# Fewer, longer vector operations and a new order for the opening of a Strassen-type matrix product on one core

## The chip, the core and the metric

The kernel runs on one core of one Trainium2 chip. The metric is the time of one execution on the device in microseconds. The engines of the core are named as the profile names them: PE (TensorE, the matmuls), DVE (VectorE), ACT (ScalarE), POOL (GpSimd) and SP (SyncE, which issues the DMAs here). They run side by side, each through its own list of instructions in order, and wait for each other by semaphores.

## The reference

```python
def reference(x, w):                       # x: 8 x 2048 x 2048, w: 2048 x 2048, float32
    cs = np.cumsum(x, axis=1)
    diff = cs - np.concatenate([zeros, cs[:, :-1, :]], axis=1)
    return np.matmul(diff, w).astype(np.float32)
```

The difference of the running sums is x itself up to rounding, so the kernel computes x times w: 16384 rows of 2048 by a 2048 x 2048 matrix.

## The kernel before

The rows of x are cut into 128 tiles of 128 rows. The depth of 2048 is cut into 16 pieces of 128 (`ko`), w into 32 pieces of 128 x 1024 floats, `w.h.ko` with h the half of the columns.

**The opening (period 0).** The first four row tiles (`PLAIN`) are multiplied plainly in bfloat16 while w arrives. Their x comes in 16 loads `first x.q.r` (depth quarter q, tile r, L249), is cast (`cast x.q.a`, a pair of tiles, L257), transposed on PE into a bank (`turn x.q.a`, L263) and copied out (`turned`, L275). Each weight piece is fetched (`w.h.ko`, L289), cast into a ring of seven buffers (`cast w.h.ko`, L310) and searched for its largest magnitude (`max w`, L297). `plain.h.r.ko` (L319) are the products; `part` takes a few of them early into a spare bank, and `left over` finishes those later. Ahead of the first products PE is given `WARM` matmuls on zeros (L358). The largest weight of all, `max`, `max of all` on POOL, `uw` and `uinv` (L447 to L454) gives one scale for the weights.

**The weights as sums.** With `uinv` the blocks B11, B21 and B22 of w (1024 x 1024 each) are stored as float16 over w's own place (`block`, L457), and the sums T1 = B12 - B11, T2 = B22 - T1, T3 = T2 - B11 and T4 = B21 - T2 are made on DVE, each in eight operations of 1024 elements (`difference` L538, `less` L581, called in `group_plain`). The place that a stored B12 would have serves as room for sums of quarters (`spare`). A second level cuts five of these blocks into quarters t11 to t22 and forms sums of quarters (`in1` to `in5`; `make_1` to `make_5`, L703 to L737), in four operations of 512 elements for each sum.

**The groups.** The other 124 tiles go in 31 groups of four. In a group the tiles g, g+1 and h = g+2, h+1 form two 2 x 2 block problems that are solved by seven products instead of eight (the names A11g, S1g, S2h and so on are blocks of x and their sums). The first group (`group_plain`, L817, period 0) uses the seven products directly. From the second on (`group`, L940, one period each), five of the products, P1 to P5, are themselves done by seven quarter products over the pair g, h (class `Quarters`, L743), with their own sums on DVE (`s1` to `s4`, `middle`, `last`) and copies on ACT (`first`, `out2`, `out4`). In the second group P1 is still done whole.

**In and out.** A row tile is loaded in two halves (`load`), its mean magnitude is found on ACT (`weigh`, `mean`) and inverted on DVE (`scale`), it is scaled to float16 on ACT (`narrow`) and transposed by a DMA (`turn`). Results are taken out of the PSUM banks by ACT (`keep`, with a scale, L617), added to by DVE (`add` and `add_one`, L629 and L633: one operation for each half of 512 columns) and stored by SP (`put`). PSUM is eight separate bank tiles, used in pairs.

**What sets the order.** `record` (L116) notes every operation under a label with its engine. At the end `emit` (L205) sorts all of them by a table `places`, written out in the file: the period times 1620 plus the label's number in the table of its period. The table has entries of its own for periods 0, 1, 2, 29, 30 and 31; all others use the entry `None`. The order on each engine, SP's queue of DMAs included, follows from that sort alone:

```python
def when(op):
    at, label = op[:2]
    own = places[at] if at in places else places[None]
    return at * PERIOD + own.get(label, 0)
```

## Time and profile before

| | us |
|---|---|
| runs | 1449.58, 1450.01, 1451.32 (median 1450.01) |
| span of the profiled execution, first to last instruction | 1449.2 |
| first product of the four plain tiles starts | 13.19 |
| DVE inverts the largest weight (`uinv`) | 60.77 |
| last matmul ends | 1444.13 |
| one group in the steady state | 44.03 |

The profiled execution gives its span alone; the runs were timed without the profiler. PE is busy for 99% of the span, DVE for 92%, ACT for 83%. A matmul row shows 0.38 us from its start to the end of its depth, but the next one starts 0.22 us after it; so a short hole between two matmuls does not show as idle time, and a longer one shows 0.16 us short. Likewise DVE and ACT operations that follow each other overlap by some 0.08 to 0.1 us. The lines of the profile stand in the prediction, where they are used.

### The profile page before, as it was taken

The page shows a single profiled execution, that of the slowest core. Times are in us where ns is not written, and L with a number is a line of the kernel's source. Part 1 is how long each engine was busy: PE and PEld are TensorE (multiplying, and loading weights), DVE is VectorE, ACT ScalarE, POOL GpSimd, SP SyncE. Part 2 cuts the span into 40 slices and gives each one's busy share as a digit, 9 for nine tenths or more (in the row PEclk, how much of TensorE's full clock was granted, in tenths as well). Part 3 has the DMA queues.
Part 4 walks back from the last instruction along what each step waited for, and adds up shares of the span by engine and source line. Part 5 has one row for each costly group of instructions (what it writes and reads, how often), then busy time and mean ns, then how long its engine had stood idle before and what let it go on. Part 6 is the DMA issues. An engine that isn't in the chain of part 4 may idle for free.

```text
span 1449.2 us, 20358 instructions
## 1 busy us (share of the span) xinstructions
PE 1438.6 (99%) x6692; PEld 652.2 (45%) x6698; DVE 1334.3 (92%) x2345; ACT 1204.5 (83%) x1994; POOL 0.5 (0%) x5
## 2 busy tenths in 40 slices
PE   8999999999999999999999999999999999999998
PEld 4444444444444444444444444444444444444443
DVE  6999999999999999999999999999999999999988
ACT  5997888898888888888988888988888888889783
POOL 0000000000000000000000000000000000000000
PEclk9999999999999999999999999999999999999999
DMA  9999979899888999989998888998989998989973
GB/s 360 369 252 272 252 212 228 240 247 262 226 234 226 243 262 231 244 222 228 247 265 233 228 229 237 252 257 226 222 239 244 260 248 225 218 236 248 264 200 116
DMA packets 343930, 351.59 MB, mean 243 GB/s; under 512 B 270992, under 2 KB 270992, under 8 KB 343824
## 3 DMA queue, kind: packets, MB, share of 16 engines
q1 hardware_dynamic: 343824, 350.29, 89.4%
q8 instruction: 52, 0.85, 0.2%
q14 instruction: 54, 0.44, 0.1%
HBM read 150.99 MB, written 134.22 MB: 197 GB/s over the span
## 4 chain that ended last, share of the span: by engine, by line
PE 91%; issue 4%; DMA 2%; ACT 2%; DVE 1%; DVEq 0%; POOLq 0%; ACTq 0%; SPq 0%
PE b L610 61%; PE b L588 30%; DMA x<-F 1%; DMA F<-in_x_dram 1%; DVE W L460 1%; ACT waste L140 0%; DMA out_dram<-arena 0%; ACT W L462 0%; DVE arena L635 0%; ACT arena L624 0%; ACT F L178 0%; ACT arena L342 0%; ACT arena L178 0%; DVE arena L576 0%; DVE W L576 0%
## 5 line engine op out<-in xcount | busy, mean ns | idle before, releaser
L588 PE MATMUL b<-W,x 128*128 128x512 f16 x2144 | 518.1, 379 | 0.1
L635 DVE SCALAR_TENSOR_TENSOR arena<-b,tiny,arena 128x512 f32<-128x512 f32 x612 | 446.9, 745 | 16.0 <-PE b L610 4.8
L610 PEld LDWEIGHTS <-arena 128*128 128x128 f16 x2744 | 268.2, 98 | 325.4 <-DVE arena L576 6.3
L610 PE MATMUL b<-W,arena 128*128 128x512 f16 x1672 | 413.7, 379 | 0.8 <-DVE arena L576 0.4
L624 ACT ACTIVATE arena<-b,tiny 128x512 f32<-128x512 f32 x496 | 317.0, 684 | 35.4 <-PE b L588 14.9
L588 PEld LDWEIGHTS <-x 128*128 128x128 f16 x2144 | 209.7, 98 | 253.3 <-issue 0.3
L140 ACT ACTIVATE waste<-F,tiny 128x1024 uint8<-128x1024 f32 x246 | 283.9, 1154 | 15.6 <-DMA F<-in_x_dram 14.1
L178 ACT ACTIVATE F<-F,tiny 128x1024 f16<-128x1024 f32 x246 | 282.1, 1147 | 10.9 <-DVE tiny L163 9.4
L610 PE MATMUL b<-W,x 128*128 128x512 f16 x1192 | 287.5, 379 | 0.0
L610 PE MATMUL b<-arena 128*128 128x512 f16 x1072 | 261.6, 379 | 0.0
L610 PEld LDWEIGHTS <-x 128*128 128x128 f16 x1428 | 139.7, 98 | 168.5
L576 DVE TENSOR_TENSOR b<-b,arena 128x512 f32<-128x512 f32 x298 | 205.9, 691 | 5.7 <-ACT arena L627 2.0
L627 ACT COPY b<-b 128x512 f32<-128x512 f32 x149 | 85.5, 574 | 134.4 <-PE b L610 112.4
L627 ACT COPY arena<-b 128x512 f32<-128x512 f32 x298 | 170.2, 580 | 19.9 <-PE b L610 13.0
L576 DVE TENSOR_TENSOR arena<-W 128x2048 f16<-128x2048 f16 (+1 forms) x158 | 185.6, 1176 | 0.4 <-PE b L610 0.4
L576 DVE TENSOR_TENSOR arena<-x,x 128x512 f16<-128x512 f16 (+1 forms) x181 | 91.5, 506 | 50.1 <-PE b L610 50.1
L576 DVE TENSOR_TENSOR x<-x,x 128x1024 f16<-128x1024 f16 x124 | 85.2, 687 | 2.0
L576 DVE TENSOR_TENSOR arena<-W,arena 128x512 f16<-128x512 f16 (+1 forms) x157 | 85.9, 563 | 0.6 <-PE b L610 0.5
L576 DVE TENSOR_TENSOR arena<-arena 128x512 f16<-128x512 f16 x120 | 50.8, 424 | 13.7 <-PE b L610 11.8
L610 PE MATMUL b<-arena,x 128*128 128x512 f16 x236 | 60.3, 379 | 0.0
L324 PE MATMUL b<-arena 128*128 128x512 bf16 x234 | 53.5, 379 | 1.5 <-DVE arena L279 0.8
L576 DVE TENSOR_TENSOR arena<-x,arena 128x512 f16<-128x512 f16 x119 | 49.6, 417 | 0.6 <-PE b L610 0.6
(49 smaller groups left out, 503.6 us busy)
## 6 DMA issues: line engine op xcount, KB each, us to landing
F<-in_x_dram SPq DMA_DIRECT2D x246, 512.0 KB, 5.4
out_dram<-arena SPq DMA_DIRECT2D x240, 512.0 KB, 4.8
W<-in_w_dram SPq DMA_DIRECT2D x31, 512.0 KB, 9.5
out_dram<-arena SPq DMA_DIRECT2D x31, 256.0 KB, 2.7
W<-in_x_dram SPq DMA_DIRECT2D x16, 256.0 KB, 6.6
x<-F SPq DMA_TRANSPOSE x246, 4.4
arena<-in_x_dram SPq DMA_DIRECT2D x2, 512.0 KB, 5.1
W<-in_w_dram SPq DMA_DIRECT2D x2, 256.0 KB, 9.0
```

The lines of the kernel that those rows point to most:

```text
L140: lambda: nc.scalar.activation(waste, data, ABS, bias=least, scale=1.0 / ROW, accum_out=m),
L178: lambda: nc.scalar.activation(to, data, COPY, scale=s),
L324: said = nc.tensor.matmul(to[n], xP[:, r, ko, :], b[:, ds(n * NB, NB)], start=(ko == 0), stop=(ko == KO - 1),)
L460: ask = lambda: nc.vector.tensor_scalar(to, src, uinv, None, MUL)
L576: record(label, "dve", lambda: nc.vector.tensor_tensor(dst, p, q, op))
L588: said = nc.tensor.matmul(to[n], a[k], b[k][:, n, :], start=(start and k == 0), stop=(k == KH - 1), skip_group_check=True,)
L610: said = nc.tensor.matmul(to, a[k], b[k], start=(start and k == 0), stop=(k == 3), skip_group_check=True)
L624: record(label, "act", lambda: nc.scalar.activation(c, p, COPY, scale=u))
L627: record(label, "act", lambda: nc.scalar.copy(to, p))
L635: label, "dve", lambda: nc.vector.scalar_tensor_tensor(c, p, u, c, MUL, ADD)
```

## The change

The diff has five parts.

1. The first-level sums T2, T3 and T4 take two depth pieces in one operation (four operations of 2048 elements in place of eight of 1024), and each sum of quarters takes the whole quarter (one operation of 2048 in place of four of 512). Additions to C take both halves in one operation of 1024 elements in periods 0 to 2, that is in the first three groups, and stay in halves from period 3 on. For this, PSUM becomes one tile of eight banks, and a pair of banks has a name for both.
2. Operations that copy or scale are recorded for either engine (`on_two`), and a list `moved` names those that change between ACT and DVE: 26 in period 0 (list below), and 3, 5 and 6 in periods 1, 2 and 3, all from ACT to DVE there.
3. Seven operations on the weights' quarters (in2, in3) stay in group 0 and nine (in1, in4, in5) in group 1, as before; the new functions `made` and `plainly` only restate when they are formed and which product is done whole (P1 of the second group, as before).
4. `WARM` is 24 in place of 30.
5. `places` has new tables for periods 0, 1 and 2 and one more for period 3, with the first loads in another order; 29, 30, 31 and `None` are as they were. The number of matmuls apart from the warm-ups is the same, and so is the number of DMAs.

```diff
-    WARM = 30
+    WARM = 24
...
-    banks = [psum.tile([P, NB], f32, name=f"b{i}") for i in range(8)]
-    pairs = [banks[2 * i : 2 * i + 2] for i in range(4)]
+    bank = psum.tile([P, 8, NB], f32, name="banks")
+    banks = [bank[:, i, :] for i in range(8)]
+
+    class Two(list):
+        def __init__(self, i):
+            super().__init__(banks[i : i + 2])
+            self.both = bank[:, ds(i, 2), :]
+
+    pairs = [Two(2 * i) for i in range(4)]
...
+    moved = {
+        0: (
+            "turned x.0.0", "cast w.0.0", "cast x.1.0", "cast x.1.1", "cast w.0.3", "part",
+            "turned x.2.0", "cast w.0.8", "cast x.3.0", "cast x.3.1", "cast w.0.9",
+            "turned x.3.0", "turned x.3.1", "cast w.0.12", "cast w.1.1", "out.0.1.0",
+            "out.0.1.1", "out.0.2.0", "out.0.2.1", "cast w.1.15", "B11.2", "B22.1", "B22.5",
+            "B22.6", "keep C22.1", "keep C12g.0",
+        ),
+        1: (
+            "narrow4.1", "narrow6.1", "keep C21g.0",
+        ),
+        2: (
+            "narrow4.1", "keep C22g.0", "keep C12h.0", "narrow6.1", "keep C21h.1",
+        ),
+        3: (
+            "keep C11g.0", "narrow4.1", "keep C12g.1", "keep C22h.1", "keep C21g.0",
+            "keep C21h.1",
+        ),
+    }
...
+        if isinstance(ask, dict):
+            if label in moved.get(period[0], ()):
+                engine = {"act": "dve", "dve": "act"}[engine]
+            ask = ask[engine]
...
+    def on_two(to, src, scale=None):
+        if scale is None:
+            return {
+                "act": lambda: nc.scalar.copy(to, src),
+                "dve": lambda: nc.vector.tensor_copy(to, src),
+            }
+        return {
+            "act": lambda: nc.scalar.activation(to, src, COPY, scale=scale),
+            "dve": lambda: nc.vector.tensor_scalar(to, src, scale, None, MUL),
+        }
...
+    def sums_of_two(dst, p, q, ks=range(0, KH, 2)):
+        for k in ks:
+            tensor(f"{dst}.{k}", *(of_two(*own[t], k) for t in (dst, p, q)), SUB)
...
     def add(label, c, p, u, halves=range(2)):
-        for n in halves:
-            add_one(f"{label}.{n}", c[:, n, :], p[n], u)
+        if period[0] > 2:
+            for n in halves:
+                add_one(f"{label}.{n}", c[:, n, :], p[n], u)
+            return
+        at = period[0], label, id(c)
+        asked[at] = asked.get(at, 0) + len(halves)
+        if asked[at] == 2:
+            add_one(label, c, p.both, u)
...
     def make_2(i):
-        t11, t12, t21, t22 = i.t
+        t11, t12, t21, t22 = i.wide.values()
         q, r, v = i.room(), i.room(), i.room()
-        less(f"{i.name}.make1", q, t12, t11)
-        less(f"{i.name}.make2", r, t22, q)
-        less(f"{i.name}.make3", t12, t22, t12)
-        less(f"{i.name}.make4", v, t21, r)
...
+        minus(f"{i.name}.make1", q, t12, t11)
+        minus(f"{i.name}.make2", r, t22, q)
+        minus(f"{i.name}.make3", t12, t22, t12)
+        minus(f"{i.name}.make4", v, t21, r)
```

The first loads on SP, in the order of the queue:

```
before: first x.0.2, x.1.1, x.0.0, x.1.3, x.0.3, x.0.1, x.1.2, x.1.0, w.0.0, w.0.1, x.2.3, w.0.2, w.0.3, w.0.4
after:  first x.0.2, x.0.0, x.1.1, x.0.1, x.0.3, x.1.0, w.0.1, w.0.0, x.1.2, w.0.2, x.1.3, w.0.3, w.0.4, w.0.5
```

Around the first group's transposing loads, the queue reads:

```
before: turn0.0, load1.0, load1.1, turn0.1, load3.0, turn2.0, load3.1, turn2.1, turn1.0, turn1.1
after:  turn0.0, turn0.1, load1.0, load1.1, put out.0.2.0, put out.1.1.1, turn2.0, turn2.1, load3.0, load3.1, turn1.0, turn1.1
```

On PE the order of the opening begins so, up to the third weight piece:

```
before: 22 warm, turn x.0.1, 7 warm, turn x.1.0, 1 warm, turn x.0.0, plain.0.1.0, plain.0.0.0, plain.0.3.0, plain.0.3.1
after:  19 warm, turn x.0.1, 3 warm, turn x.0.0, turn x.1.0, 2 warm, plain.0.2.0, plain.0.2.1, plain.0.0.0, plain.0.3.0
```

More of the change, by code (lines that the diff above doesn't have):

```diff
@@ L277, in turned @@
         v = v.rearrange("p (r c) -> p r c", r=2)
-        on = nc.scalar.copy if engine == "act" else nc.vector.tensor_copy
-        record(f"turned x.{q}.{a}", engine, lambda: on(to, v))
+        record(f"turned x.{q}.{a}", engine, on_two(to, v))
     wb = {}
@@ L458, in block @@
         to, src = dst[k], whole[k][:, a, h, :].rearrange("p (n c) -> p n c", c=NB)
-        if engine == "dve":
-            ask = lambda: nc.vector.tensor_scalar(to, src, uinv, None, MUL)
-        else:
-            ask = lambda: nc.scalar.activation(to, src, COPY, scale=uinv)
-        record(f"{name}.{k}", engine, ask)
+        record(f"{name}.{k}", engine, on_two(to, src, uinv))
     def finish_row(r):
@@ L972, in group @@
         P1.slot(1)
-        if more:
+        if not P1.plain:
             in_1.give("Q4")
```

180 lines of the change are left out of this document (107 added, 73 removed), and 482 rows, old and new, of the table places.

## The prediction

> **What bounds the kernel now.** I read the page's head and busy shares first, then the windows of each stretch, the chain of waits, TensorE's waits, and last the engines' rows in order of time.
>
> ```profile
> span 1449.2 us, 20358 instructions
> PE 1438.6 (99%) x6692; PEld 652.2 (45%) x6698; DVE 1334.3 (92%) x2345; ACT 1204.5 (83%) x1994; POOL 0.5 (0%) x5
> PE 91%; issue 4%; DMA 2%; ACT 2%; DVE 1%; DVEq 0%; POOLq 0%; ACTq 0%; SPq 0%
> ```
> ```profile
> 166.25 13.81 PE b L610 x64
> ```
> ```profile
> 1.17 6.24 PE L362 MATMUL b<-arena 128*128 128x512 bf16 x22 [1.17 <-DVE arena L237]
> 9.09 0.62 PE L269 MATMUL b<-waste,W 128*128 128x128 bf16 x8 [1.68 <-DVE W L260]
> 13.19 4.30 PE L324 MATMUL b<-arena 128*128 128x512 bf16 x17 [0.79 <-DVE arena L279]
> 41.84 2.53 PE L324 MATMUL b<-arena 128*128 128x512 bf16 x10 [0.34 <-ACT arena L313]
> 136.99 1.02 PE L610 MATMUL b<-W,arena 128*128 128x512 f16 x4 [0.40 <-ACT b L627]
> 138.45 1.90 PE L610 MATMUL b<-W,arena 128*128 128x512 f16 x8 [0.44 <-DVE arena L576]
> 1443.10 1.03 PE L610 MATMUL b<-W,x 128*128 128x512 f16 x4
> ```
>
> TensorE bounds the kernel and runs at its pace: 64 products in 13.81 us, 0.2158 us each. There are 6698 weight loads, so 6698 matmuls; 30 are warm-ups and 64 short transposes, which leaves 6604 products of 512 columns: 6604 x 0.2158 = 1425.1 us. The first starts at 13.19, the last ends at 1443.10 + 1.03 = 1444.13, which is 1430.9 us. The 40 transposes in between take (0.62 - 0.22) / 7 = 0.06 each, 2.3 in all. So 1430.9 - 1425.1 - 2.3, less 0.2 for the last one's depth, is **3.3 us of holes in the whole run**. The two holes at 137 us are the largest: 0.40 and 0.44 idle, each 0.16 longer in pace, because a matmul shows 0.38 us and gives way after 0.22; together 1.2 us.
>
> That is the size of the game. The diff leaves the number of products alone (the program has 12 fewer TensorE instructions, six warm-ups with their weight loads) and doesn't touch the order of the last groups, so the 5.1 us behind the last product stay. Only two things can shrink: the 13.19 us ahead of the first product, and the 3.3 us of holes.
>
> **The first loads.** The DMA engines are full here (405 GB/s below), so a load's place in the queue, in bytes, sets when it lands.
>
> ```profile
> 8.34 0.69 DVE L260 CAST W<-W 128x1024 bf16<-128x1024 f32 x1 [5.08 <-DMA W<-in_x_dram]
> ```
> ```profile
> 11.57 1.05 ACT L313 CAST arena<-W 128x1024 bf16<-128x1024 f32 x1 [9.57 <-DMA W<-in_w_dram]
> 14.81 1.04 ACT L313 CAST arena<-W 128x1024 bf16<-128x1024 f32 x1 [0.34 <-DMA W<-in_w_dram]
> 16.09 1.04 ACT L313 CAST arena<-W 128x1024 bf16<-128x1024 f32 x1 [0.23 <-DMA W<-in_w_dram]
> 17.37 1.04 ACT L313 CAST arena<-W 128x1024 bf16<-128x1024 f32 x1 [0.23 <-DMA W<-in_w_dram]
> ```
>
> Casts that wait for weights follow each other by 1.28 us, the time of 512 KB. `first x.0.3`, which releases `cast x.0.1` at 8.34, is fifth in both orders. `w.0.0` was ninth, behind eight loads of 256 KB; now it is eighth, behind six of them and `w.0.1`: the same 2.5 MB, so it lands at 11.57 again. In the old order the first product did not wait for that but for the third turned piece of x on VectorE. Now ScalarE takes `cast x.1.0` and `turned x.0.0`, and VectorE is free to cast `w.0.0`: 11.57 + 0.69 + 0.06 to the reader = 12.3 instead of 13.19. **Gain 0.9** (the six warm-ups dropped count for nothing, since TensorE sat 1.68 us idle behind them); bounds 0 (something else arrives last) and 1.6 (`w.0.0` landing when `w.0.1` now does, 1.28 earlier).
>
> From there TensorE would meet `plain.1.3.0` after 117 products and 40 transposes, at 12.3 + 25.2 + 2.3 = 39.8, against 41.84. It passes the landings of the last quarters `w.0.12` to `w.0.15` with no time in hand, so I leave 0.4 us of holes there.
>
> **Fewer, longer operations.** Counted in the two programs: 24 sums T2, T3, T4 of 1024 elements become 12 of 2048, 64 quarter sums of 512 become 16 of 2048, and 50 additions to C of 512 become 25 of 1024.
>
> ```profile
> L635 DVE SCALAR_TENSOR_TENSOR arena<-b,tiny,arena 128x512 f32<-128x512 f32 x612 | 446.9, 745 | 16.0 <-PE b L610 4.8 <-ACT arena L627 4.6 <-ACT arena L624 2.0
> L576 DVE TENSOR_TENSOR arena<-W 128x2048 f16<-128x2048 f16 x150 | 182.4, 1216 | 0.4 <-PE b L610 0.4
> L576 DVE TENSOR_TENSOR W<-W 128x512 f16<-128x512 f16 x44 | 17.2, 417 | 0.1
> L576 DVE TENSOR_TENSOR W<-W 128x1024 f16<-128x1024 f16 x24 | 15.5, 683 | 0.1
> L543 DVE SCALAR_TENSOR_TENSOR W<-W,tiny 128x1024 f16<-128x1024 f32 x8 | 9.9, 1276 | 0.0
> L460 DVE TENSOR_SCALAR W<-W,tiny 128x1024 f16<-128x1024 f32 x18 | 12.2, 748 | 0.1
> L340 DVE COPY arena<-b 128x512 f32<-128x512 f32 x2 | 1.4, 680 | 0.0
> ```
> ```profile
> 77.48 4.85 DVE L543 SCALAR_TENSOR_TENSOR W<-W,tiny 128x1024 f16<-128x1024 f32 x4
> 98.73 3.09 DVE L576 TENSOR_TENSOR W<-W 128x1024 f16<-128x1024 f16 x5
> 116.35 0.75 DVE L576 TENSOR_TENSOR arena<-W 128x512 f16<-128x512 f16 x2
> 1442.93 2.73 DVE L635 SCALAR_TENSOR_TENSOR arena<-b,tiny,arena 128x512 f32<-128x512 f32 x4
> ```
>
> Neighbours overlap, so the engine's time is from start to start, not the duration. An addition takes (2.73 - 0.74) / 3 = 0.66; a 1024 sum (3.09 - 0.68) / 4 = 0.60; a 512 sum 0.75 - 0.42 = 0.33; the 2048 sum 1.22 less the same 0.08 = 1.13. An addition of 1024 out of PSUM is in no row; the nearest is the 1024 form of that operation out of SBUF, (4.85 - 1.28) / 3 = 1.19. Saved: 25 x (1.32 - 1.19) = 3.3, 12 x (1.20 - 1.13) = 0.8, 16 x (1.32 - 1.13) = 3.0. **VectorE saves 7 us**, bounds 0 (a form over two weight tiles or two banks takes its parts' time) and 14 (the durations' own differences). I take 7, the start-to-start rows.
>
> A price that only a page states: by the Trainium skill, VectorE: DVE Perf Modes, section on the TRN2 errata, an operation out of PSUM costs 120 cycles plus one per element at 0.96 GHz; an estimate from it is 1.19 us for the addition of 1024, so the sum would be the same.
>
> That the banks are now one tile, and that `on_two` can ask either engine, is no instruction: 0. The merged additions wait for both halves of a product. Where halves stood side by side (132.63 and 133.29 us in group 1) nothing is lost. Behind `C11g+P2.g` now stand `P2.last`, `S1h`, `S3h` and `P5.s1`, for which product `P5.1` waits.
>
> **The moves between ScalarE and VectorE.** After the weights' scale is known (61 us), VectorE takes 11 evacuations (`keep`: 2 in group 0, 1, 3, 5) and 5 `narrow` (0, 2, 2, 1) from ScalarE; four blocks change sides, two each way. A `keep` costs VectorE 0.60 (copy of 512 out of PSUM, 0.68 less the overlap) to 0.66 (the addition), a `narrow` 0.66 (0.75 less 0.08): 11 x 0.60 + 5 x 0.66 = 9.9 us. ScalarE loses as much or more.
>
> ```profile
> 14.00:43.00 29.00, 28.40 (x158) 13.80 (x159) 22.68 (x24) 23.34 (x27) 0.00 (x0) 1.00 1.03 405
> 61.00:100.00 39.00, 38.70 (x180) 17.30 (x179) 38.82 (x60) 38.05 (x59) 0.00 (x0) 1.00 0.95 266
> 100.00:138.00 38.00, 37.55 (x173) 16.65 (x171) 35.98 (x83) 28.59 (x49) 0.00 (x0) 1.00 1.11 265
> 138.00:182.00 44.00, 43.56 (x203) 19.74 (x203) 43.24 (x88) 37.02 (x62) 0.00 (x0) 1.00 0.93 252
> 182.00:226.00 44.00, 44.00 (x206) 19.97 (x204) 42.50 (x76) 36.91 (x64) 0.00 (x0) 1.00 0.84 224
> 226.00:270.00 44.00, 44.00 (x206) 19.94 (x204) 40.72 (x73) 37.42 (x63) 0.00 (x0) 1.00 0.92 246
> 270.00:314.00 44.00, 44.00 (x206) 19.91 (x205) 40.72 (x73) 37.45 (x64) 0.00 (x0) 1.00 0.89 238
> ```
>
> (Columns: length; busy time of PE, PEld, DVE, ACT, POOL with instruction counts; clock, DMA share, GB/s.) VectorE is busy 38.82 + 35.98 + 43.24 + 42.50 + 40.72 = 201.3 of the 209 us from 61 to 270; only 7.7 are idle. It gets 9.9 - 7.1 = **2.8 us more** there: less in group 0 (-1.7) and 1 (-1.0), more in group 2 (+1.8) and 3 (+3.7, where nothing is merged). In group 3 that makes 40.72 + 3.7 = 44.4 us of work for 44.0. Ahead of 61 us it gets seven weight casts, a copy and two turned pieces and gives up four casts of x, 6 x 0.61 (0.69 less 0.08) = 3.7 us, into 6.3 idle ones (29 - 22.68); so the maximum of the weights, and with it `uinv`, comes when it came.
>
> Does VectorE then deliver in time? From the first weight block to `P5.s2` of group 1 the new order has 18 blocks (0.66), 8 T1 and 8 additions (1.19), 13 sums of x (0.60), 25 long sums (1.13) and 6 us of small things: 73 us, so `P5.s2` is done at 61 + 73 = 134. Its reader `P5.2` comes after 556 products and 40 transposes, at 12.3 + 120.0 + 2.3 = 134.6. Before, that pair met at 138.45 with a hole. So **the two holes at 137 can go**, and VectorE is just early enough for a TensorE that is 2 to 4 us ahead.
>
> **What is late next.** On SyncE, `turn2.0` now stands behind `put out.1.1.1`, which waits for ScalarE's `out.1.1.1`.
>
> ```profile
> L140 ACT ACTIVATE waste<-F,tiny 128x1024 uint8<-128x1024 f32 x246 | 283.9, 1154 | 15.6 <-DMA F<-in_x_dram 14.1
> L178 ACT ACTIVATE F<-F,tiny 128x1024 f16<-128x1024 f32 x246 | 282.1, 1147 | 10.9 <-DVE tiny L163 9.4
> L342 ACT COPY arena<-b 128x512 f32<-128x512 f32 x13 | 7.0, 585 | 0.0
> x<-F SPq DMA_TRANSPOSE x246, 4.4
> ```
> ```profile
> 59.56 1.14 ACT L140 ACTIVATE waste<-F,tiny 128x1024 uint8<-128x1024 f32 x1
> 60.83 1.15 ACT L140 ACTIVATE waste<-F,tiny 128x1024 uint8<-128x1024 f32 x1
> ```
>
> Ahead of it ScalarE has four weighings, three narrowings, a block, five copies and some small ones: 4 x 1.27 (start to start, 60.83 - 59.56) + 3 x 1.06 + 1.06 + 5 x 0.5 (durations less 0.08) + 0.8 = 12.6 us. It started this list at 59.56, when the last weight cast was done, and starts it there again, so `out.1.1.1` comes at about 72. A transposing load lands 4.4 us after its issue, 76.4; `A11h B11`, which reads it, comes after 284 products and 40 transposes, at 12.3 + 61.3 + 2.3 = 76, and may wait up to 0.8.
>
> Together with the start I count 0.8 of holes up to 90 us and 1.2 for the rest (what the pair at 137 was, now somewhere in groups 1 to 3, where VectorE is full): 2.0 against 3.3. **Sum: 0.9 + 1.3 = 2.2 us; span 1449.2 - 2.2 = 1447.0.** The runs' median 1450.01 stands 0.8 above the span, so 1447.8 us.
>
> **The rivals.**
> 1. All holes go: -0.9 - 3.3 = 1445.8. For: the sums above meet their readers. Against: every margin is a few tenths. 0.15.
> 2. The change does not do what it says: the start is swallowed by the landings at 38 us and the work moved to VectorE opens as much as it closes: 1450.0. For: a VectorE that is full from 61 us on gets more work, and the landings at 36 us are where they were. Against: the pair at 137 meets with 4 us less. 0.17.
> 3. VectorE becomes the bound: it cannot close its 7.7 us of waits, so its extra 2.8 us come out in TensorE, and the start's gain is spent waiting for it: 1450.0 + 2.8 = 1452.8. It decides once VectorE's idle time from 61 to 270 stays above 7.7 - 2.8 = 4.9. For: group 3's 44.4 of 44.0. Against: the groups behind it have 44 - 40.72 = 3.3 idle us each. 0.13.
> 4. The clock falls back. The first 22 matmuls took 6.24 us where 22 x 0.2158 is 4.75: some ran slowly. With three warm-ups fewer ahead of the first transpose the 1.68 idle us become 2.3. If slow matmuls came back once, 1.3 us: 1449.1. 0.05. The Trainium skill, TensorE: Matmul & The Clock Gate, Part 1, says that a whole idle window of about 3.4 us halves the clock; the trace agrees that 1.68 does not, and by the page 2.3 would not either.
>
> **How the numbers follow.** Forecast 0.50, own range 1446.6 to 1449.0. The range 1445.5 to 1451.2 leaves out about half of rivals 1 and 3 and a little more. 0.2% is 2.9 us, about what a measurement of this kernel can tell from no change. Below 1447.1: rival 1 and two fifths of the forecast, 0.34. Above 1452.9: half of rival 3 and unforeseen holes, 0.10. Between: 0.56.
>
> **What would show it.** First product at 12.3 and `plain.1.3.0` near 40.2; no hole near 135; VectorE idle under 5 us from 61 to 270; TensorE's holes 2.0. A first product past 13, or holes that wait for VectorE after 180 us, would make the prediction wrong.

## The result and the profile after

The changed kernel takes 1460.17 us (median; 1459.85 to 1461.02), the kernel before 1450.25 on the same chip (1449.58 to 1451.32): a ratio of 1.0070, 95% interval 1.0058 to 1.0082, so 9.9 us slower. The span of its profiled execution is 1458.4 us, 9.2 above before's.

The head of the page after, its first busy line and the shares of the chain:

```profile
span 1458.4 us, 20265 instructions
...
PE 1441.9 (99%) x6686; PEld 652.5 (45%) x6692; DVE 1340.2 (92%) x2282; ACT 1187.5 (81%) x1972; POOL 0.9 (0%) x5
...
PE 89%; DMA 4%; DVE 3%; ACT 2%; issue 1%; SPq 0%; DVEq 0%; ACTq 0%
```

VectorE's busy time is only 5.9 us higher than before, ScalarE's 17 lower. What grew in the chain is DMA (2% to 4%) and VectorE (1% to 3%): TensorE waits more often, for engines that are not busier. The windows after, with the columns of those before (length; busy of PE, PEld, DVE, ACT, POOL with counts; clock, DMA share, GB/s):

```profile
0.00:14.00 14.00, 9.24 (x47) 4.72 (x48) 4.95 (x13) 3.27 (x3) 0.19 (x4) 0.89 0.83 285
...
61.00:100.00 39.00, 37.96 (x174) 16.71 (x174) 37.32 (x53) 37.37 (x58) 0.71 (x1) 1.00 0.95 253
100.00:138.00 38.00, 38.00 (x177) 17.20 (x176) 37.68 (x44) 26.78 (x45) 0.00 (x0) 1.00 1.03 263
138.00:182.00 44.00, 40.14 (x176) 17.23 (x175) 37.61 (x58) 30.94 (x55) 0.00 (x0) 0.96 0.81 222
182.00:226.00 44.00, 43.78 (x202) 19.55 (x201) 40.91 (x67) 32.05 (x56) 0.00 (x0) 1.00 0.81 226
226.00:270.00 44.00, 43.57 (x202) 19.33 (x200) 43.42 (x79) 32.84 (x55) 0.00 (x0) 1.00 0.82 227
270.00:314.00 44.00, 43.42 (x201) 19.43 (x200) 40.01 (x72) 36.71 (x64) 0.00 (x0) 1.00 0.91 240
314.00:358.00 44.00, 44.00 (x205) 19.96 (x204) 40.73 (x73) 37.45 (x64) 0.00 (x0) 1.00 0.93 242
```

Read the counts of matmuls: 138 to 182 has 176 where before had 203, that is 27 x 0.2158 = 5.8 us of products missing, and the granted clock is 0.96. VectorE, meant to be full there, was busy 37.61 of 44. From 314 on nothing is lost. What TensorE loses is measured here from the start of one matmul to the start of the next, as time beyond the 0.2158 us of its pace; a hole, here and below, is such a loss at one place. By that measure the 9.2 us are: 0.7 handed on at 71 us by the late start, 0.9 more than before between 80 and 100, 0.3 less around 138, **5.5 between 164 and 175** and 2.5 between 182 and 314; together 9.3.

**The start.** TensorE and VectorE after, in order of time (start, length, instructions, and in brackets the idle time ahead and its releaser):

```profile
1.31 5.57 PE L394 MATMUL banks<-arena 128*128 128x512 bf16 x19 [1.31 <-DVE arena L275]
10.33 0.63 PE L307 MATMUL banks<-waste,W 128*128 128x128 bf16 x8 [3.44 <-DVE W L157]
10.79 1.45 PE L394 MATMUL banks<-arena 128*128 128x512 bf16 x3
12.04 2.04 PE L307 MATMUL banks<-waste,W 128*128 128x128 bf16 x16
13.87 0.78 PE L394 MATMUL banks<-arena 128*128 128x512 bf16 x2
14.48 1.03 PE L361 MATMUL banks<-arena 128*128 128x512 bf16 x3
```
```profile
9.58 1.30 DVE L157 CAST W<-W 128x1024 bf16<-128x1024 f32 x2 [6.51 <-DMA W<-in_x_dram]
```

`cast x.0.1` waits for `first x.0.3` until 9.58 instead of 8.34. TensorE idles 3.44 us instead of 1.68, and behind that three warm-ups take 1.45 us and 16 transposes 2.04. That is about half speed: in e2 below three warm-ups take 0.81 and eight transposes 0.62. The first product starts at 14.48, 1.3 us later than before and 2.2 later than I said.

**Group 1.** The three engines around the largest loss:

```profile
161.13 2.75 PE L625 MATMUL banks<-W,x 128*128 128x512 f16 x12
...
165.74 1.03 PE L625 MATMUL banks<-W,x 128*128 128x512 f16 x4
169.85 1.02 PE L647 MATMUL banks<-W,arena 128*128 128x512 f16 x4 [3.08 <-DVE banks L613]
170.98 1.67 PE L647 MATMUL banks<-arena 128*128 128x512 f16 x4
172.44 3.85 PE L647 MATMUL banks<-W,x 128*128 128x512 f16 x12
```
```profile
166.58 1.28 DVE L680 SCALAR_TENSOR_TENSOR arena<-banks,tiny,arena 128x1024 f32<-128x1024 f32 x1 [4.09 <-ACT arena L160]
167.78 0.42 DVE L613 TENSOR_TENSOR arena<-x,arena 128x512 f16<-128x512 f16 x1
...
168.45 0.74 DVE L161 TENSOR_SCALAR arena<-banks,tiny 128x512 f32<-128x512 f32 x1
169.11 0.69 DVE L613 TENSOR_TENSOR banks<-banks,arena 128x512 f32<-128x512 f32 x1
```
```profile
163.12 1.15 ACT L182 ACTIVATE waste<-F,tiny 128x1024 uint8<-128x1024 f32 x1 [2.94 <-DMA F<-in_x_dram]
...
164.73 1.15 ACT L182 ACTIVATE waste<-F,tiny 128x1024 uint8<-128x1024 f32 x1
...
165.87 0.67 ACT L160 ACTIVATE arena<-banks,tiny 128x512 f32<-128x512 f32 x1
```

Read it backwards. `P4.5` waits 3.08 us for `P4.middle` (169.11). That stands on VectorE behind the merged addition `C22g+X`, ahead of which VectorE sat idle for 4.09 us until ScalarE's `keep C21g.1` (165.87) was done. The keep reads one of the two banks X that the addition reads; and the keep stood behind `weigh7.0` and `weigh7.1`, of which the first waited 2.94 us for its load. Behind the hole eight matmuls are slow: twelve take 3.85 us at 172.44 and took 2.75 at 161.13. Before, the addition was in two halves that stood apart in the order. `C22g+X.1` (the second of the two additions at 158.94) ran ahead of the keep, and `C22g+X.0` (the first of the two at 163.32) stood behind `P4.middle` (162.72), so nothing that TensorE waited for stood behind the keep. VectorE before:

```profile
158.94 1.39 DVE L635 SCALAR_TENSOR_TENSOR arena<-b,tiny,arena 128x512 f32<-128x512 f32 x2
...
162.72 0.69 DVE L576 TENSOR_TENSOR b<-b,arena 128x512 f32<-128x512 f32 x1
163.32 1.40 DVE L635 SCALAR_TENSOR_TENSOR arena<-b,tiny,arena 128x512 f32<-128x512 f32 x2
```

### The profile page after: what moved, and what is told of

Same layout as the page of the kernel before. It is cut to its first block, busy times and chain, and to the rows that moved or that the text cites. A ratio compares the mean times of both kernels' runs of the same rounds, so it can differ in the third digit from the quotient of the medians.

```text
span 1458.4 us, 20265 instructions
## 1 busy us (share of the span) xinstructions
PE 1441.9 (99%) x6686; PEld 652.5 (45%) x6692; DVE 1340.2 (92%) x2282; ACT 1187.5 (81%) x1972; POOL 0.9 (0%) x5
## 4 chain that ended last, share of the span: by engine, by line
PE 89%; DMA 4%; DVE 3%; ACT 2%; issue 1%; SPq 0%; DVEq 0%; ACTq 0%
PE banks L647 58%; PE banks L625 27%; PE banks L361 3%; DMA F<-in_x_dram 2%; DMA x<-F 1%; DVE arena L613 1%; DVE arena L680 1%; ACT waste L182 1%; DVE W L613 1%; ACT arena L160 0%; DMA W<-in_x_dram 0%; ACT F L160 0%; DVE x L613 0%; DMA x<-arena 0%; PE banks L307 0%
## 5 line engine op out<-in xcount | busy, mean ns | idle before, releaser
L625 PE MATMUL banks<-W,x 128*128 128x512 f16 x2144 | 518.7, 379 | 0.2 <-DVE x L613 0.2
L680 DVE SCALAR_TENSOR_TENSOR arena<-banks,tiny,arena 128x512 f32<-128x512 f32 (+1 forms) x587 | 443.1, 769 | 21.1 <-ACT arena L160 8.0
L647 PE MATMUL banks<-W,arena 128*128 128x512 f16 x1672 | 414.1, 379 | 4.6 <-DVE banks L613 3.5
L160 ACT ACTIVATE arena<-banks,tiny 128x512 f32<-128x512 f32 x485 | 310.4, 684 | 34.5 <-PE banks L625 14.3
L647 PE MATMUL banks<-W,x 128*128 128x512 f16 x1192 | 289.4, 380 | 0.0
L647 PE MATMUL banks<-arena 128*128 128x512 f16 x1072 | 263.0, 380 | 0.5 <-ACT banks L156 0.2
L613 DVE TENSOR_TENSOR banks<-banks,arena 128x512 f32<-128x512 f32 x298 | 206.2, 692 | 5.9 <-ACT arena L156 2.6
L156 ACT COPY arena<-banks 128x512 f32<-128x512 f32 (+1 forms) x315 | 181.6, 586 | 34.6 <-PE banks L647 17.5
L156 ACT COPY banks<-banks 128x512 f32<-128x512 f32 x149 | 85.5, 574 | 135.8 <-PE banks L647 114.7
L613 DVE TENSOR_TENSOR arena<-W 128x2048 f16<-128x2048 f16 x152 | 184.9, 1217 | 0.3 <-PE banks L647 0.2
L647 PE MATMUL banks<-arena,x 128*128 128x512 f16 x236 | 60.4, 379 | 0.0
```

Of the source, the lines that this page charges most:

```text
L156: "act": lambda: nc.scalar.copy(to, src),
L160: "act": lambda: nc.scalar.activation(to, src, COPY, scale=scale),
L613: record(label, "dve", lambda: nc.vector.tensor_tensor(dst, p, q, op))
L625: said = nc.tensor.matmul(to[n], a[k], b[k][:, n, :], start=(start and k == 0), stop=(k == KH - 1), skip_group_check=True,)
L647: said = nc.tensor.matmul(to, a[k], b[k], start=(start and k == 0), stop=(k == 3), skip_group_check=True)
L680: label, "dve", lambda: nc.vector.scalar_tensor_tensor(c, p, u, c, MUL, ADD)
```

## Experiments

Each is an edit of the changed kernel (keys in `places` unless said). The ratio is to the kernel before in the same set of runs, with its 95% interval; the changed kernel itself is 1.0070 (1.0058 to 1.0082). "Back" means the difference of two such ratios, in us. For e2 and e3 that difference is smaller than the uncertainty, and for e1, e9 and e12 the intervals overlap a little, so there the rows of the traces carry the argument.

| run | us | ratio |
|---|---|---|
| e1_add_first | 1457.49 | 1.0046 (1.0029 to 1.0063) |
| e2_loads_before | 1459.27 | 1.0061 (1.0046 to 1.0076) |
| e3_warm36 | 1459.65 | 1.0065 (1.0050 to 1.0080) |
| e4_no_moves | 1464.84 | 1.0100 (1.0085 to 1.0116) |
| e5_weigh_late, e8_w_behind_x | 1459.46, 1460.78 | one execution each |
| e6_halves | 1455.56 | 1.0038 (1.0023 to 1.0053) |
| e7_put_first | 1455.78 | 1.0039 (1.0026 to 1.0051) |
| e9_three_fixes | 1456.91 | 1.0046 (1.0031 to 1.0061) |
| e10_groups_2_3_before | 1454.83 | 1.0035 (1.0021 to 1.0049) |
| e11_put_late | 1451.84 | 1.0016 (1.0007 to 1.0025) |
| e12_groups_2_3_alone | 1457.40 | 1.0050 (1.0036 to 1.0063) |
| e13_more_warm | 1451.60 | 1.0010 (1.0001 to 1.0019) |
| e14_cast_back | 1451.27 | 1.0008 (0.9999 to 1.0017) |
| e15_weigh_behind_keep | 1452.37 | 1.0016 (1.0007 to 1.0026) |

### The stall of group 1: e1, e5, e7, e6

```diff
+    places[1]['keep C21g.1'] = -1334.5
```

> The changed kernel with one place altered: in group 1 the merged addition C22g+X stands ahead of ScalarE's keep C21g.1, which reads the same two banks, and no longer behind it. Theory A (the long stall of 166.4 to 170.3 us is this one wait, 4.09 us of VectorE behind a ScalarE list that itself waits for a load, and the clock falls back behind it): C22g+X starts near 162.5 instead of 166.58, P4.middle ends near 166, the hole of 3.25 us before P4.5 shrinks to under 0.5, no product behind it is at 0.427 us, and the time falls by 4 to 5 us, to 1455.2 to 1456.2. Rival (VectorE has too much to do between 138 and 182, and whatever wait is taken away, another operation is late): the hole moves to another product and at most 1.5 us come back, 1458.7 or more.

VectorE of this run:

```profile
162.43 1.28 DVE L680 SCALAR_TENSOR_TENSOR arena<-banks,tiny,arena 128x1024 f32<-128x1024 f32 x1
...
166.09 0.75 DVE L161 TENSOR_SCALAR arena<-banks,tiny 128x512 f32<-128x512 f32 x1 [1.72 <-DMA out_dram<-arena]
```

The addition now runs at 162.43, the hole before `P4.5` shrinks to 0.5 and the slow products are gone, as theory A said. TensorE loses 2.1 us between 164 and 175 instead of 5.5. But 3.5 us came back, not 4 to 5, and the trace shows a second wait: the next keep (`keep C21g.0`, on VectorE since the change) waits 1.72 us for a DMA out of `arena`. That is `put0.1`, which still reads the buffer that the keep is to fill. On SP's queue it now stands behind `load7.0` and `load7.1`, and lands at 165.65 in the changed kernel (160.37 before). So `keep C21g.1`, which fills the other half of that buffer, may have had two causes of its lateness that ended within 0.2 us of each other; the next two runs part them.

```diff
+    places[1].update({'weigh7.0': -1334.9, 'weigh7.1': -1334.8})
```

> The changed kernel with weigh7.0 and weigh7.1 of group 1 behind keep C21g.1 and C22g+X in ScalarE's order, so that the keep no longer stands behind a load. Two theories of why C22g+X came 4.09 us late. A1 (ScalarE's order: the keep stands behind two weighs that wait for load7): the keep starts near 161.9, C22g+X near 162.6, the hole before P4.5 goes from 3.25 to under 0.5, time near 1455.5. A2 (the keep's buffer: put0.1 still reads it until 165.65, since it stands behind load7.0 and load7.1 on the queue; it happens to land 0.2 us before the weighs end): the keep starts at 165.5 to 166.2 again, the hole stays at 3 us or more, and with the weighs behind it the time stays at 1459.5 to 1461.5.

ScalarE of this run, and then of the next, e7, which adds this line:

```diff
+    places[1].update({'load7.0': -1339.8, 'load7.1': -1339.7})
```

> As the run with the weighs behind the keep, and load7.0 and load7.1 of group 1 behind put0.1 on SP's queue, as they stood in the kernel before; C22g+X stays behind the keep and stays merged. Theory A2 (the keep waited for its buffer, and ScalarE's order alone is only half of the wait): put0.1 lands near 160.4 instead of 165.65, keep C21g.1 starts by 162.6, C22g+X by 163.3, P4.middle ends near 166.7, the hole before P4.5 falls from 3.25 to 0.3 to 0.9, the eight slow products go, time 1455.0 to 1457.0. Theory A1 (ScalarE's order alone): the same time as the run with the weighs moved alone, within 0.5 us. Rival (VectorE's load): 1459 or more in both.

```profile
164.25 0.69 ACT L160 ACTIVATE arena<-banks,tiny 128x512 f32<-128x512 f32 x1 [3.72 <-DMA out_dram<-arena]
```
```profile
161.94 0.69 ACT L160 ACTIVATE arena<-banks,tiny 128x512 f32<-128x512 f32 x1
```

TensorE of e7 at the same place:

```profile
165.57 1.03 PE L625 MATMUL banks<-W,x 128*128 128x512 f16 x4
166.44 1.03 PE L647 MATMUL banks<-W,arena 128*128 128x512 f16 x4
...
168.16 2.75 PE L647 MATMUL banks<-W,x 128*128 128x512 f16 x12
```

With the weighs moved alone the keep waits 3.72 us for the store instead, which lands at 164.23 in this one execution, and the hole stays (3.3). With the store ahead of the loads as well, the keep runs at 161.94, the hole is gone, twelve products take 2.75 us again, and 4.5 us are back. A2 is right: **the keep had two late releasers, and removing the weighs alone left the hole as it was.** The store alone was not moved.

```diff
-            return at * PERIOD + own.get(label, 0)
+            return at * PERIOD + own.get(label, own.get(label[:-2], 0))
...
-        if period[0] > 2:
+        if period[0] > 0:
```

> The changed kernel with the additions to C of groups 1 and 2 in halves again, each half at the place in the order of the merged one (12 and 13 additions of 0.74 us twice instead of 1.28 once, about 3 us more for VectorE in each group by the spacing of 0.65 a half against 1.20). Theory A (the merging itself made the stall: a merged addition waits for whatever the other half waits for): the half C22g+X.1 goes ahead of keep C21g.1 at 162.5, the half .0 has another bank, the hole before P4.5 falls from 3.25 to under 0.6, the slow products go, and the time falls by 3 to 5 us, to 1455.2 to 1457.2. Rival (merging pays in VectorE's time what it costs in waits): the hole goes, but the extra operations open as many holes elsewhere, and the time stays within 1 us of the changed kernel's.

VectorE and ScalarE of this run:

```profile
161.48 1.40 DVE L680 SCALAR_TENSOR_TENSOR arena<-banks,tiny,arena 128x512 f32<-128x512 f32 x2
```
```profile
164.57 0.67 ACT L160 ACTIVATE arena<-banks,tiny 128x512 f32<-128x512 f32 x1
```

Both halves run at 161.48, though the keep is late here too (164.57): `.1` stands ahead of it in the order, and `.0`, which stands behind it, reads the other bank. The hole before `P4.5` is 0.5, no product behind it is slow, and 4.6 us are back (1.0038), as theory A said. VectorE does more work in more operations, and the kernel is faster. So the stall took two things together, an addition that waits for the keep and a keep that is late. e1 (the addition first) and e6 (halves) take away the one, e7 the other, and each brings the hole down to 0.5 us or less.

### The moved keeps: e4

```diff
-        1: (
-            "narrow4.1", "narrow6.1", "keep C21g.0",
-        ),
-        2: (
-            "narrow4.1", "keep C22g.0", "keep C12h.0", "narrow6.1", "keep C21h.1",
-        ),
-        3: (
-            "keep C11g.0", "narrow4.1", "keep C12g.1", "keep C22h.1", "keep C21g.0",
-            "keep C21h.1",
-        ),
```

> The changed kernel with the eleven keeps and five narrows of groups 1 to 3 back on ScalarE at their places in the order; merged operations and everything else stay. Theory A (order and waits, not load, cost the time): VectorE has about 10 us less to do and idles about as much more; the wait of C22g+X for ScalarE stays or grows, since keep C21g.0 then also stands on ScalarE; the time is within 2 us of the changed kernel's, 1458.2 to 1462.2. Rival (the 9.9 us of moved work make VectorE the bound of groups 1 to 3): the holes of 219 to 280 and most of the one at 166 go and the time falls by 4 to 7 us, to 1453 to 1456.

The edit takes back nine keeps and five narrows; the other two of the eleven keeps belong to group 0 and stay moved. It is 4.4 us slower than the changed kernel (1.0100 against 1.0070), not level and not faster. TensorE's waits for ScalarE, which were 0.4 us in the whole trace of the changed kernel, come to 6.1 us between 61 and 300 us here. So the order of the table needs the moves; which list or load makes ScalarE late in it, no run parts. The rival, that VectorE's added work in groups 1 to 3 is the cost, falls.

### The start: e2, e8, e3

```diff
+    first = ('first x.0.2', 'first x.1.1', 'first x.0.0', 'first x.1.3', 'first x.0.3',
+             'first x.0.1', 'first x.1.2', 'first x.1.0', 'w.0.0', 'w.0.1')
+    places[0].update((name, 0.5 + 0.01 * i) for i, name in enumerate(first))
```

> The changed kernel with the first nine loads, and w.0.1 behind them, in the order of the kernel before. Theory B (the late start comes from the order of the first loads: x.0.3 landed at 9.48 us instead of 8.24): x.0.3 lands near 8.24 and w.0.0 near 11.55 again, TensorE idles about 2.2 us instead of 3.44, the transposes stay at 0.056 us each, the first product starts at 13.0 to 13.5 instead of 14.48, and the time falls by 0.8 to 1.5 us, to 1458.7 to 1459.4. Rival (one DMA queue of sixteen fell behind by chance at that moment, whatever the order): x.0.3 lands at 9.3 to 9.6 again, or the changed kernel's own order lands at 8.2 in the other runs of this set, and the time stays within 0.7 us of the changed kernel's.

```profile
8.89 0.62 PE L307 MATMUL banks<-waste,W 128*128 128x128 bf16 x8 [1.51 <-DVE W L157]
...
12.50 0.62 PE L307 MATMUL banks<-waste,W 128*128 128x128 bf16 x8 [1.90 <-ACT W L156]
...
13.39 1.03 PE L361 MATMUL banks<-arena 128*128 128x512 bf16 x4
```

`first x.0.3` lands at 8.04, the transposes run at full speed, the first product starts at 13.39 instead of 14.48; 1.3 us are back, within the intervals. It is the order, not chance: in the eight kernels here with the changed order the last of a load's sixteen parts comes 2.9 to 4.1 us after the first for `x.0.3`, with the old order 1.3 to 2.0 (also eight kernels).

e8 has the same list, but with the changed order of the first six x and `w.0.0`, `w.0.1` behind all eight:

> The changed kernel with its own order of the first six loads of x, but the other two loads of x ahead of w.0.1 and w.0.0, as in the kernel before. In every run so far with the changed order of the first loads the last part of x.0.3 came 2.9 to 3.9 us behind its first, and 1.3 to 1.7 us with the order of before. If the two loads of weights in seventh and eighth place are the cause, x.0.3 lands near 8.2 here; if the order of the first six loads of x is, it lands at 9.4 to 10.1 again. Its time says little, since w.0.0 comes 1.3 us later in the order.

`x.0.3` lands at 8.15 in this one execution, its parts 1.7 us apart. So the order of the x ahead of it does not by itself make it late, and the two loads of weights behind it in the queue have a part in it. But the load after it, `x.1.0`, lands at 9.85 here with its parts 2.4 us apart, where the sixth load of the old order has 1.25 to 1.8; so the lateness is smaller and one load later rather than gone. By what means a load behind delays one ahead, no run shows.

```diff
-    WARM = 24
+    WARM = 36
+    places[0].update((f'warm.{i}', 21.5) for i in range(24, 36))
```

> The changed kernel with twelve more warm-up products ahead of the first transposition, 2.6 us of work in the 3.44 us that TensorE stood idle there. Theory (the clock fell because of the idle 3.44 us; in the kernel before the idle was 1.68 us and it held): transpositions at 0.056 us again instead of 0.106, no warm-up at 0.427, granted clock of the first 14 us 1.00 instead of 0.89, first product at 13.9 instead of 14.48 (it then waits for the cast of w.0.0, which lands at 13.15), the time 0.4 to 1.0 us lower, 1459.2 to 1459.8. Rival (the clock of the start costs nothing, since the first product waits for w.0.0 and its cast anyway): first product at 14.4 to 14.5, time as the changed kernel's within 0.2 us.

The clock holds at 1.00 and the first product is at 14.36, but `w.0.0` lands 0.4 us later in this execution. Behind that landing the first product comes after 0.8 us, and in the changed kernel after 1.3: the theory's gain, hidden by a later load. The time is 0.7 us lower by the ratios, inside both intervals. So the fall of the clock costs about half a microsecond at the first product, and the loads' order, which also made the idle time behind which the clock fell, costs the rest: with it put back (e2) the first product is 1.1 earlier and the clock holds.

### What is left: e12, e9, e10, e11, e13, e14, e15

e12 gives groups 2 and 3 the order of before from the tenth operation of group 2 on, their additions in halves and no moves; five operations of group 1 that fall into that time (two loads, a store, a transposing load and a small one on ScalarE) go back to their places of before with them:

```diff
-        if period[0] > 2:
+        if period[0] > 1 and not (period[0] == 2 and label == 'C21h+P4.h'):
...
+    places[1].update({'turn7.1': 2253, 'put3.1': 2218, 'load8.1': 2216, 'load10.0': 2260, 'unit5': 2165})
+    places[2] = group_2
+    del places[3]
```

> The changed kernel with one part undone alone: from the tenth operation of group 2 on the order of before, additions in halves and no moved keeps in groups 2 and 3; first loads, groups 0 and 1 as changed. Theory (the new order of groups 2 and 3 loses 2.2 to 4.5 us by itself): the time falls by 2 to 4 us, to 1456.2 to 1458.2, and TensorE is busy 43.8 to 44.0 of 44 us from 182 on but for the stall that group 1 hands on. Rival (the lateness of group 1 makes the holes behind it, so that nothing is won while its stall stands): 1459.5 or more.

```profile
182.00:226.00 44.00, 44.00 (x206) 19.90 (x205) 41.62 (x76) 36.68 (x62) 0.00 (x0) 1.00 0.79 208
226.00:270.00 44.00, 44.00 (x205) 19.79 (x204) 40.95 (x73) 37.14 (x63) 0.00 (x0) 1.00 0.99 247
```

TensorE is full from 182 us on, though the stall of group 1 still stands ahead of it, and 2.9 us are back. So these holes belong to what the change did to groups 2 and 3 (their order, merged additions and moves, which no run takes apart) and not to lateness handed on.

e9 joins e2 and e7 and adds one line; e10 joins e9 and e12:

```diff
+    places[0].update({'load3.0': 171.8, 'load3.1': 171.9})
```

> The changed kernel with three places put right together: the first loads in the order of before, load3.0 and load3.1 ahead of put out.1.1.1 (they stood ahead of turn1.0 and turn1.1 and held these up, so that S1g waited 1.23 us at 85), and in group 1 load7 behind put0.1 with the weighs behind the keep. Theory (the losses are separate waits that the new order makes, and they add): about 1.0 us at the start, 1.2 us at 86 and 4.4 us at 166 come back, and the time is 1453.0 to 1454.5; what is left are the holes of groups 2 and 3, 4 to 5 us. Rival (VectorE or the queues are so full in groups 0 to 3 that a wait taken away comes back behind): 1455 or more, no better than the repair of group 1 alone, 1455.8.

> As the run with three places put right, and from the tenth operation of group 2 on the order of before: its additions in halves, its keeps and narrows all on ScalarE in groups 2 and 3. Merged sums, blocks, additions and moved keeps stay in groups 0 and 1. Theory (groups 2 and 3 lose 4 to 5 us by their new order alone, since the same groups had no hole in the kernel before with the same work in smaller operations): TensorE is busy 43.8 to 44.0 of 44 us between 182 and 314, and the time is 1448.5 to 1450.5, at most level with before. Rival (what is lost there is owed to the lateness that group 1 hands on, whatever the order): holes of 2 us or more stay between 182 and 314 and the time is 1452 or more.

Both miss in time. TensorE of e10 shows one reason:

```profile
75.83 1.67 PE L618 MATMUL banks<-W,x 128*128 128x512 f16 x7
79.70 2.55 PE L618 MATMUL banks<-W,x 128*128 128x512 f16 x11 [2.20 <-DMA x<-F]
```

With `load3` ahead of `turn2`, `S1g` is in time at 86, but `A11h` waits 2.20 us for `turn2`. In groups 2 and 3 TensorE is full, as expected. This profiled execution took 1451.81 us, the other four 1454.75 to 1455.49, so it doesn't show all that they lost. The profiled one of e9 has the same hole at 79, and its clock stood at half speed for 3.4 us twice, from 13.9 and from 82.1 us. e11 is e10 with that line replaced:

```diff
+    places[0]['put out.1.1.1'] = 182.5
```

> As the run with groups 2 and 3 in the order of before, but load3 is back at the place that the change gave it, and put out.1.1.1 stands behind turn1.1 instead. In the run before, load3 ahead of turn2.0 closed the hole at 86 but opened one of 2.36 us at 78, where A11h waited for turn2. Theory (SP's queue was the cause in both places, and a store of 1.05 us is the thing to move there): no hole over 0.5 us at 78 and under 0.5 at 86, TensorE's losses in all 9 to 10 us against 11.8, time 1448 to 1451, level with before or a little faster. Rival (the queues of 61 to 100 are full, and whatever is moved something is late): a hole of 1 us or more at 78 or at 86, 1452 or more.

No hole at 78 or 86; 1.0016. `turn1.1` lands at 83.87, where it landed at 86.32 in the changed kernel, with the loads `load3` ahead of it landing at 81.04 instead of 84.47. The time is above the expected range by 0.8, and single executions lie between 1450.99 and 1454.87. The four slowest of the eleven, from 1452.97 on, are those whose granted clock over the execution is 0.998; the others have 0.999 or 1.000. Two more runs on the start, e13 (twelve warm-ups in its two idles) and e14 (six, and `cast x.1.0` back on VectorE):

> As the run with all places put right, with twelve more warm-up products, six in each of the two idles of about 2 us ahead of the first product. Theory (the fall of the clock in some executions makes the scatter): the clock is 1.00 in all executions, these lie within 1.5 us of each other instead of 3.9, the median falls by 0.5 to 1.0 us, to 1450.8 to 1451.4; the first product stays at 13.4 to 13.7, since it waits for other engines. Rival (the scatter comes from elsewhere): the executions still lie over 3 us apart, the median is at 1451.6 to 1452.2.

> As the run with all places put right, with six more warm-up products ahead of the first transposition, and cast x.1.0 on VectorE behind turned x.0.1 instead of on ScalarE. Theory (the first product waits for the transposition of x.1.0, which ScalarE's late cast holds up to 12.9 us): that transposition starts at 11.0 to 11.6, the first product at 12.2 to 12.7 instead of 13.7, and the time falls by 0.8 to 1.5 us, to 1450.3 to 1451.0 or 0.3 us lower where the clock also holds, level with the kernel before. Rival (the first product waits for w.0.0, which lands at 11.3 to 11.7 and must be cast, and what comes early is caught up at the next load): the first product is earlier by at most 0.5 us and the time is 1451.3 or more.

e13's clock is 0.999 or 1.000 in all eleven executions, and they still scatter from 1450.21 to 1453.67, with the median at the rival's 1451.6. So the clock is at most a part of the scatter: the theory falls. e14's first product starts at 12.34, where I had put it, and ScalarE gives it back: the products behind wait for its cast of `w.0.1`, which lands at 12.61, and then for its copy of turned x:

```profile
12.34 0.59 PE L354 MATMUL banks<-arena 128*128 128x512 bf16 x2
13.73 0.59 PE L354 MATMUL banks<-arena 128*128 128x512 bf16 x2 [0.80 <-ACT arena L149]
14.65 1.68 PE L354 MATMUL banks<-arena 128*128 128x512 bf16 x7 [0.32 <-ACT arena L149]
```

e14 has the lowest median of all, level with the kernel before (1.0008, 0.9999 to 1.0017); its interval overlaps those of e11, e13 and e15. In e13's profiled execution 2.8 us of holes stood between 114 and 139. e15 tried one cause on e14:

```diff
+    places[0].update({'weigh7.1': 227.5, 'mean7': 227.6})
```

> As the run with cast x.1.0 back on VectorE, with weigh7.1 and mean7 of group 0 behind the two keeps of C21 on ScalarE. There weigh7.1 waits for load7.1, which lands at 118 to 120 us, and products that need the keeps' banks stand behind it (holes of 0.4 to 0.8 us at 120 to 123 in several runs, none where TensorE came late). Theory (a weigh behind a late load, ahead of keeps, is the same fault as in group 1, and its cost changes from execution to execution with the loads): no hole over 0.2 us between 110 and 130, executions within 1.8 us of each other, median 0.5 to 1.0 us lower, 1450.2 to 1450.8. Rival (the holes there have another cause, such as VectorE): they stay, and the median is 1451.0 to 1451.5.

It misses: the executions lie within 1.9 us, but 1.1 us higher, which the intervals don't tell from e14. The hole at 121 is gone, and there are others, of 0.3 to 0.8 us, between 114 and 139. Ahead of them VectorE stands 2.15 us at 111 behind a `weigh5.1` whose load landed late.

```profile
113.26 0.16 DVE L198 RECIPROCAL tiny<-tiny 128x1 f32<-128x1 f32 x1 [2.15 <-ACT tiny L196]
```

What sets the last 1 to 2 us of these versions, and their scatter, stays open. No version here beats the kernel before. e14 still has the merged sums and additions and the moves of groups 0 and 1, so the work that these save on VectorE bought no time that these runs can show.

## Why the prediction was wrong, point by point

The forecast was 1447.8 us, 2.2 faster; the measured time is 9.9 slower. The sum had a gain at the start and a gain in the holes, and set almost nothing for the waits that the new order makes.

- **The bound and the tail: right.** Full TensorE at 0.2158 us per product; nothing changes behind 314 us. All of the loss is holes and slow products.
- **First loads: the step that failed first.** That `first x.0.3` "is fifth in both orders", and so releases its cast at 8.34 again, took a load's landing from the bytes ahead of it. The rest of the order counts too (e2), in part the loads behind it (e8): the landing let the cast start at 9.58, and `w.0.0` landed at 13.15 instead of 11.55. The gain of 0.9 us at the first product became a loss of 1.3, of which 0.7 was left at 71 us. And where e14 did start at 12.34, the waits for the next cast and copy on ScalarE ate it.
- **Warm-ups "count for nothing": true only with the loads in time.** In e2, with 24 warm-ups and the old order of loads, TensorE idles 1.51 us and the clock holds. With the late load the idle became 3.44 us, not 2.3, and the clock did fall. Twelve more warm-ups (e3) kept it up and brought the first product about half a microsecond nearer to the landing of `w.0.0`.
- **Sizes of the merged operations: right.** The row of the 25 additions and one of the long sums:

```profile
L680 DVE SCALAR_TENSOR_TENSOR arena<-banks,tiny,arena 128x1024 f32<-128x1024 f32 x25 | 31.7, 1279 | 6.3 <-ACT arena L160 6.2
L613 DVE TENSOR_TENSOR W<-W 128x2048 f16<-128x2048 f16 x23 | 27.4, 1217 | 0.1
```

  An addition takes 1.20 from start to start (166.58 to 167.78; said: 1.19). The work saved was real. But the first row shows the price that I set at nothing: 6.3 us of idle time ahead of these 25 operations, 6.2 of it behind ScalarE's keeps.
- **"The merged additions wait for both halves of a product", priced at nothing: the step that cost most.** I checked one addition, `C11g+P2.g`. I did not follow `C22g+X`, whose halves stood apart with a keep on the same bank between them. That was 5.5 us at 164 to 175, of which e6, with the additions of groups 1 and 2 in halves, gives 4.6 back, and e7, with the keep in time, 4.5. The late keep was the other half of this step: I followed neither `put0.1` past `load7` on the queue nor the keep past the weighs.
- **The moves: sized right, judged wrong.** VectorE idled 209 - 196.9 = 12.1 us between 61 and 270, above rival 3's mark of 4.9, yet it is not the bound: without the moves of groups 1 to 3 the kernel is 4.4 us slower. Idle time of an engine that waits is not room.
- **`P5.s2` against `P5.2`: wrong by what lay ahead.** One of the two holes is there again, 0.6 us at 138. VectorE had lost 1.23 at 85 waiting for `turn1`, which stood behind a store and `load3` on the queue, and the start was late; but e1 and e6, with the same hole of 1.0 us at 86, have none at 138, so what makes it stays open. I had followed `turn2` past the store and not `turn1` past the loads. And `turn2.0` was in time by luck: it landed at 77.97, not 76.4, 0.25 us ahead of its reader, which came late itself.
- **"1.2 for the rest" of the holes: too small by about 8.** Besides the 5.5 in group 1, groups 2 and 3 lost 2.5, by e12 through what the change did to them, and the wait at 85 cost 0.9 more than before.
- **Rival 4 came true twice:** at the start, and in a place that I had not named, behind the hole of group 1, where it cost 1.7 us, eight products at 0.427 instead of 0.2158.

## What to carry to other kernels

When two operations become one, the one waits for everything that either waited for, and blocks all that stands behind it in order: list for each merged operation which other engine touches any bank or buffer of it, and what that engine waits for at that point. When an order is written anew, follow each store and load past its neighbours on the queue: a store behind two loads keeps a buffer, and with it a keep, an addition and a product. And take away all releasers of a stall that end together before judging any one of them.

## What the runs showed of the hardware

- Two engines that only read the same bank were kept in turn. The addition `C22g+X` waited 4.09 us for ScalarE's keep, which reads one of its two banks; in e6 the half on the other bank did not wait. The Trainium skill, PSUM — Partial Sum Buffer, section "PSUM bank collisions raise a hardware error", says that two engines may not access one bank (in the same quarter of its partitions) at once, "ScalarE-read with VectorE-read included", and that programs have to guard banks by semaphores. The trace agrees that this program does; no run here lets the two collide.
- Idle time did not settle by its length whether the clock fell. It fell behind 3.08 us (after, at 170) and 2.05 (e7, ahead of its first transposes, eight of which then took 1.04 us), and held behind 3.16 (e5, at 168) and 2.54 (e5, at the start).

```profile
10.47 1.04 PE L307 MATMUL banks<-waste,W 128*128 128x128 bf16 x8 [2.05 <-DVE W L157]
```
```profile
168.25 1.02 PE L647 MATMUL banks<-W,arena 128*128 128x512 f16 x4 [3.16 <-DVE banks L613]
...
170.25 2.75 PE L647 MATMUL banks<-W,x 128*128 128x512 f16 x12
```

  What did settle it is the place of the idle time. In these traces the granted clock is full or half, and every stretch of one clock but the last is a multiple of 3.41 us, so it changes only at marks 3.41 us apart. In the changed kernel one such mark is at 171.23, 1.4 us after TensorE was back at work (clock in the third column from the end):

```profile
167.82:171.23 3.41, 1.28 (x6) 0.52 (x7) 3.41 (x8) 0.96 (x3) 0.00 (x0) 1.00 0.76 215
171.23:174.65 3.42, 3.42 (x10) 1.22 (x9) 2.81 (x5) 1.94 (x3) 0.00 (x0) 0.50 0.86 228
```

  Over all 17 traces the clock fell eleven times, each time at the end of a stretch between two marks in which TensorE stood idle for 1.90 to 3.14 of the 3.41 us; in no other stretch, from the clock's first rise to the last matmul, did it idle longer than 1.91. The 3.16 us of e5 were cut by a mark, 1.90 ahead of it and 1.25 behind.

  The Trainium skill, TensorE: Matmul & The Clock Gate, Part 1, says that the clock is judged in free-running windows of 3.4 us and falls after an idle one; that the place in the window matters agrees with these rows, and the eight slow products (8 x 0.427 = 3.4 us) agree with its length. That a window must be idle throughout does not: about 1.9 of 3.41 us were enough.
